# Gate and up of a decoder block: seven half-size products for each pair of tiles in place of eight

## The chip, the cores and the metric

The kernel runs on one core of one Trainium2 chip. The metric is the device time of one execution in microseconds (us), lower is better; the number given is the median of three runs. The engines are named as the profile names them: PE (matmuls; PEld are its weight loads), DVE (VectorE), ACT (ScalarE), POOL (GpSimd), SP (which issues most transfers). Each engine works through its own list of instructions in order and waits on semaphores for the others.

## The reference

One decoder block over 512 tokens of width 1024: a first norm, one wide projection, two token mixers (a retention with decay and a softmax attention with forget gates), a gated merge and an output product, then the feed-forward part, which is what the change touches:

```python
x = x + merged @ w_out[l]
h2 = rmsnorm(x, g_ffn[l])
ff = (jax.nn.silu(h2 @ w_gate[l]) * (h2 @ w_up[l])) @ w_down[l]
x = x + ff
```

`w_gate` and `w_up` are 1024 x 2816, `w_down` is 2816 x 1024, all in float32. 2816 columns are 22 tiles of 128, or 11 pairs of tiles, for gate and for up each.

## The kernel before

All stages have features on the 128 partitions and tokens along the free axis where it helps. Every float32 factor of a product is split into a high part (a cast to fp32r, on ACT) and a low part (the float32 value less its high part, on DVE), and each product is three matmuls: high x high, high x low, low x high (`three`, issued in line L72). A weight block is loaded by SP (L143), cast by ACT (L150, `wh<-raw`) and subtracted by DVE (L151, `wl<-raw,wh`).

The parts that matter here come last in the program, one behind the other:

- **The o-stage**: four pairs of output tiles of `merged @ w_out`, each pair 48 matmuls of 128x512. Behind each tile DVE adds x (L681), ACT scales by g_ffn and casts into `xgh` (L682), DVE makes `xgl` (L683), ACT squares (L685, L688), and POOL adds the squares up into `sqs` (L689). The scaled x is not yet divided by its root mean square: that factor, `r2` (one value for each token, spread over 128 partitions), comes later, as it goes through the products unchanged.
- **Gate/up**: 22 half rounds, in turn a pair of gate tiles and a pair of up tiles, each 2 tiles x 8 blocks of 128 features x 3 = 48 matmuls of 128x512. Gate: DVE multiplies the PSUM tile by `r2` (L705), ACT takes Silu (L706). Up: DVE multiplies by `r2` (L711), POOL multiplies by the gate and writes `pf` (L712). In the first round one more matmul of ones by `sqs` makes the sums of squares in all partitions, and DVE works out `r2` on 128x512 tiles.
- **Down**: 22 blocks k; each is loaded and split, `pf[k]` is split (L740 on ACT, L741 on DVE) and goes through 24 matmuls of 128x512 into eight PSUM tiles; the last two blocks are taken tile by tile, with the output added and stored behind each tile (L751, L752).

Pools of SBUF buffers set how far ahead a load can be: raw weight blocks have two or three buffers, so a load waits for the subtraction that last read its buffer. `tile.TileContext` places instructions on each engine by its own model of when they are due; where `pinned[0]` is set, PE's matmuls keep the order in which the code names them.

## Time and profile before

| what | value |
|---|---|
| runs | 733.34, 733.04, 733.48 us (median 733.34) |
| profiled execution, its own time | 733.68 us |
| span of its profile | 731.8 us |
| o-stage, first to last matmul's start | 323.7 to 367.2 us of the span |
| gate/up | 367.2 to 607.5 us (240.3 us) |
| down and output | 607.5 us to the end |
| PE busy / DVE / ACT / POOL | 99% / 50% / 35% / 15% of the span |

A line of a group reads: source line, engine, operation, out<-in by the program's names, shapes, count, then the busy time in us and the mean ns of one, then the idle time of that engine just before these instructions and what ended it. A line of the timeline reads: start in us, duration, engine, line, operation, names, shape, count, and in brackets the idle time before it. A matmul's duration is its modelled time from issue to result; how fast matmuls follow each other is read from the differences of their starts. A line of waits reads: who waited for whom, us in total, number of waits, the longest.

### The profile page before, as it was taken

How to read it: one execution, taken by the hardware profiler on the slowest of the kernel's cores; microseconds unless marked ns; L12 is line 12 of the kernel's file. 1: busy time of each engine (PE TensorE's matmuls, PEld its weight loads, DVE VectorE, ACT ScalarE, POOL GpSimd, SP SyncE). 2: the span in 40 equal slices, each digit the busy share in tenths (PEclk: the TensorE clock that was granted, in tenths of full speed). 3: DMA queues.
4: the chain of work that ended last, by engine and by line, in shares of the span. 5: the costliest groups of instructions: out<-in, count | busy, mean ns of one | idle time of the engine just before them, and what ended most of it. 6: DMA issues, size and time to landing. Idle time of an engine off the chain costs nothing.

```text
span 731.8 us, 8835 instructions
## 1 busy us (share of the span) xinstructions
PE 724.0 (99%) x3433; PEld 594.2 (81%) x3433; DVE 363.7 (50%) x630; ACT 259.1 (35%) x389; POOL 111.7 (15%) x112
## 2 busy tenths in 40 slices
...
GB/s 280 241 123 89 79 62 90 81 134 99 86 87 30 58 113 89 89 102 212 96 139 140 89 112 88 96 106 88 103 98 86 114 88 86 108 93 88 86 0 116
DMA packets 23353, 76.20 MB, mean 104 GB/s; under 512 B 2696, under 2 KB 3080, under 8 KB 23312
## 3 DMA queue, kind: packets, MB, share of 16 engines
...
q8 instruction: 27, 0.44, 0.3%
q14 instruction: 14, 0.11, 0.0%
q10 hardware_dynamic: 144, 0.02, 0.0%
HBM read 73.52 MB, written 2.11 MB: 103 GB/s over the span
## 4 chain that ended last, share of the span: by engine, by line
PE 94%; DVE 2%; ACT 1%; DMA 1%; issue 1%; POOL 0%; DVEq 0%; SPq 0%; ACTq 0%
PE acc L72 78%; PE sc L72 8%; PE tp L72 6%; PE tp L75 2%; DVE pr L494 1%; DMA xf<-in_xT_dram 1%; DMA raw<-in_w_tok_dram 0%; POOL cb L486 0%; DVE pr L498 0%; DVE tq L473 0%; ACT pr L496 0%; DVE kl L464 0%; ACT tk L463 0%; DVE up L711 0%; DVE pl L741 0%
## 5 line engine op out<-in xcount | busy, mean ns | idle before, releaser
L150 ACT CAST wh<-raw 128x1024 fp32r<-128x1024 f32 (+1 forms) x118 | 123.8, 1052 | 378.6 <-PE acc L72 313.9
L151 DVE TENSOR_TENSOR wl<-raw,wh 128x1024 fp32r<-128x1024 f32 (+1 forms) x118 | 152.2, 1291 | 196.7 <-ACT wh L150 195.3
L72 PE MATMUL acc<-xgh,wh 128*128 128x512 f32 x352 | 137.3, 390 | 0.0
L72 PE MATMUL acc<-xgh,wl 128*128 128x512 f32 x352 | 136.9, 389 | 0.0
L72 PE MATMUL acc<-xgl,wh 128*128 128x512 f32 x352 | 136.9, 389 | 0.0
L72 PEld LDWEIGHTS acc<-xgl,wh 128*128 128x128 f32 x352 | 66.1, 188 | 14.0 <-issue 0.2
L72 PEld LDWEIGHTS acc<-xgh,wl 128*128 128x128 f32 x352 | 66.1, 188 | 13.9
L72 PEld LDWEIGHTS acc<-xgh,wh 128*128 128x128 f32 x352 | 66.1, 188 | 13.8 <-issue 0.2
L72 PE MATMUL acc<-wh,xh 128*128 128x512 f32 (+2 forms) x192 | 69.7, 363 | 0.1
L712 POOL TENSOR_TENSOR pf<-up,gt 128x512 f32<-128x512 f32 x22 | 38.3, 1758 | 199.3 <-DVE up L711 199.3
L72 PE MATMUL acc<-wh,xl 128*128 128x512 f32 (+2 forms) x192 | 68.2, 355 | 0.0
L72 PE MATMUL acc<-wl,xh 128*128 128x512 f32 (+2 forms) x192 | 68.0, 354 | 0.0
L72 PE MATMUL acc<-xh,wh 128*128 128x512 f32 x128 | 51.8, 404 | 0.0
L72 PE MATMUL acc<-xh,wl 128*128 128x512 f32 x128 | 50.0, 391 | 0.0
L72 PE MATMUL acc<-xl,wh 128*128 128x512 f32 x128 | 49.9, 390 | 0.0
L72 PEld LDWEIGHTS acc<-wh,xh 128*128 128x128 f32 x192 | 36.2, 188 | 6.1 <-issue 0.5
L72 PEld LDWEIGHTS acc<-wh,xl 128*128 128x128 f32 x192 | 36.2, 189 | 5.2
L72 PEld LDWEIGHTS acc<-wl,xh 128*128 128x128 f32 x192 | 36.2, 189 | 4.6
L72 PE MATMUL acc<-pl,wh 128*128 128x512 f32 x88 | 34.2, 389 | 0.0
L72 PE MATMUL acc<-ph,wl 128*128 128x512 f32 x88 | 34.2, 389 | 0.0
L72 PE MATMUL acc<-ph,wh 128*128 128x512 f32 x88 | 33.9, 389 | 0.0
L689 POOL TENSOR_TENSOR sqs<-sqs,sq 128x512 f32<-128x512 f32 x7 | 11.6, 1651 | 122.2 <-ACT sq L688 122.0
...
## 6 DMA issues: line engine op xcount, KB each, us to landing
raw<-in_w_gu_dram SPq DMA_DIRECT2D x44, 512.0 KB, 3.5
raw<-in_w_dn_dram SPq DMA_DIRECT2D x22, 512.0 KB, 3.5
raw<-in_w_tok_dram SPq DMA_DIRECT2D x16, 512.0 KB, 3.6
raw<-in_w_a_dram SPq DMA_DIRECT2D x16, 512.0 KB, 3.6
raw<-in_w_y_dram SPq DMA_DIRECT2D x8, 512.0 KB, 3.6
raw<-in_w_o_dram SPq DMA_DIRECT2D x8, 512.0 KB, 3.9
...
```

Source lines behind the costliest of these rows:

```text
L72: in_order(nc.tensor.matmul(o, **kw))
L75: in_order(nc.tensor.transpose(out=o, in_=src, identity=ident))
L150: nc.scalar.copy(out=h[:, :width], in_=raw[:, :width])
L151: tt(out=l[:, :width], in0=raw[:, :width], in1=f32(h)[:, :width], op=ALU.subtract)
L494: nc.vector.tensor_tensor_reduce(out=pr[:, :n], in0=cb[:, :n], in1=sc[:, :n], scale=-1.0, scalar=3e38, op0=ALU.add, op1=ALU.min, accum_out=nm)
L689: gp.tensor_tensor(out=sqs, in0=sqs, in1=sq2, op=ALU.add)
L712: gp.tensor_tensor(out=pf[:, 2 * f2 + m2, :], in0=up, in1=gts[m2], op=ALU.mult)
```

## The change

Of a pair of tiles the product is a 2x2 block product: x is cut into quarters by token half and by even or odd feature block (A11, A12, A21, A22), the weights by feature block and tile (B11 ... B22). Eight products of half size were done as 48 matmuls of 128x512. The change does seven (Strassen's scheme in Winograd's form), each over four feature blocks and three split terms, so 7 x 12 = 84 matmuls of 128x256 for a pair. With

S1 = A21 - A22, S2 = S1 - A11, S3 = A11 - A21, S4 = S2 + A12 and T1 = B12 + B11, T3 = B12 + B22, T2 = T1 + B22, T4 = T2 + B21,

the seven products are B11 by A11, T1 by S1, T2 by S2, B21 by A12, T3 by S3, B22 by S4, T4 by A22; sums of them give the four quarters of the result (the first, for one, is y + u0, with y = B21 by A12 and u0 = B11 by A11). All minus signs sit in the S's, so the weights are only added.

- **o-stage**: the evacuation writes the scaled float32 x into `fx` (eight quarter slots, L695) and not straight into a high and a low part; DVE makes S1 to S4 (L705 to L708); the high and low parts of seven slots are made by two casts (L685) and two subtractions (L686) for each pair of tiles. `sq2`, the squared tile, has one buffer in place of two.
- **Weights, `factors`**: SP loads B12 twice into the two slots of `t13` (L734, 512 KB) and the other three blocks into `raw` (L735, 768 KB); POOL issues a transfer that adds B11 and B22 onto `t13` (L736, 512 KB, once the first load has landed; two of the four sums, T1 and T3, are made so); DVE makes T2 and T4 (`t24`, L740, L741). Casts (L727) and subtractions (L728) make high and low parts of `raw` (`ah`, `al`, 128x1536), `t13` (`ch0`, `cl0`, 128x1024) and `t24` (`ch1`, `cl1`, 128x1024). `raw`, `t13`, `ah`, `al` have two buffers each, in two pools; the second pool (`fp`) lies where the o-stage's buffers were. `t24`, `ch0`, `cl0`, `ch1`, `cl1` have one.
- **Sums of products**: three PSUM tiles x, y, z per pair; between the products ACT copies 128x256 states of x and z to SBUF (u0 L765, u3 L767, u1 L770, u2 L773, and the last one L775), and DVE makes the other three quarters (L779 to L781).
- **The rest of gate/up**: gate by `r2` in one 128x1024 multiply (L816; L812 for the first), Silu 128x1024 (L817; L813 for the first); up is multiplied by the gate on DVE (L820, 128x1024); POOL does no arithmetic in this stage. `r2` comes from four 128x1 matmuls after pair 0, a short chain of DVE on 128x4, and, after pair 1, four transposes of PE that spread it (`broadcast_cols`, L233 and L75). PE's order is pinned.
- **Down**: up's factor `r2` is now multiplied here (L843, one 128x512 on DVE for each k); the buffers are those of the gate/up stage (`hl` in those of `xfh`).

```diff
-    hp = tc.alloc_tile_pool(name="hp", bufs=1, side="left")
+    hp = tc.alloc_tile_pool(name="hp", bufs=1, side="right")
...
+    HT = S // 2
...
-    xgh = xp.tile([P, NK, S], F32R, name="xgh")
-    xgl = xp.tile([P, NK, S], F32R, name="xgl")
+    xfh = [xp.tile([P, 7, HT], F32R, name="xfh", tag=f"xfh{j}") for j in range(4)]
+    xfl = [xp.tile([P, 7, HT], F32R, name="xfl", tag=f"xfl{j}") for j in range(4)]
+    wq = tc.alloc_tile_pool(name="wq", bufs=1, side="right")
+    tmp = tc.alloc_tile_pool(name="tmp", bufs=1, side="left")
+    sqs = r1
+    A11, A12, A22, S1, S2, S3, S4, A21 = range(8)
+    def split_x(j, f, lo, hi):
+        nc.scalar.copy(out=xfh[j][:, lo:hi, :], in_=f[:, lo:hi, :])
+        tt(out=xfl[j][:, lo:hi, :], in0=f[:, lo:hi, :], in1=f32(xfh[j])[:, lo:hi, :], op=ALU.subtract)
+
     for mp in range(4):
+        fx = tmp.tile([P, 8, HT], F32, name="fx", tag="fx")
         def evac_o(m2, acc):
             m = 2 * mp + m2
             xn = x1[:, m, :]
             tt(out=xn, in0=acc, in1=xn, op=ALU.add)
-            act(out=xgh[:, m, :], in_=xn, func=AF.Copy, scale=gffn(m))
-            stt(out=xgl[:, m, :], in0=xn, scalar=gffn(m), in1=f32(xgh)[:, m, :], op0=ALU.mult, op1=ALU.subtract)
+            act(out=fx[:, 0:8:7, :] if m2 == 0 else fx[:, 1:3, :], in_=xn.rearrange("p (s t) -> p s t", s=2), func=AF.Copy, scale=gffn(m))
             if m == 0:
                 act(out=sqs, in_=xn, func=AF.Square)
             else:
-                sq2 = xp.tile([P, S], F32, name="sq2", tag="sq2", bufs=2)
+                sq2 = tmp.tile([P, S], F32, name="sq2", tag="sq2")
                 act(out=sq2, in_=xn, func=AF.Square)
                 gp.tensor_tensor(out=sqs, in0=sqs, in1=sq2, op=ALU.add)
         run(feat(lambda u: w_o[mp, u], 2, mgh, mgl, evac_o))
+        split_x(mp, fx, 0, 3)
+        tt(out=fx[:, S1, :], in0=fx[:, A21, :], in1=fx[:, A22, :], op=ALU.subtract)
+        tt(out=fx[:, S2, :], in0=fx[:, S1, :], in1=fx[:, A11, :], op=ALU.subtract)
+        tt(out=fx[:, S3, :], in0=fx[:, A11, :], in1=fx[:, A21, :], op=ALU.subtract)
+        tt(out=fx[:, S4, :], in0=fx[:, S2, :], in1=fx[:, A12, :], op=ALU.add)
+        split_x(mp, fx, 3, 7)
+    B12, B11, B21, B22 = range(4)
+    wpools = [wq]
+    WT = {"raw": (3, F32), "t13": (2, F32), "t24": (2, F32), "ah": (3, F32R), "al": (3, F32R),
+          "ch0": (2, F32R), "cl0": (2, F32R), "ch1": (2, F32R), "cl1": (2, F32R)}
+    seen = {}
+    def wtile(tag):
+        n, dt = WT[tag]
+        two = tag in ("raw", "t13", "ah", "al") and len(wpools) > 1
+        i = seen.get(tag, 0)
+        seen[tag] = i + 1
+        return wpools[i % 2 if two else 0].tile([P, n, 512], dt, name=tag, tag=tag)
+    def split_to(src, tags):
+        h, l = wtile(tags[0]), wtile(tags[1])
+        nc.scalar.copy(out=h, in_=src)
+        tt(out=l, in0=src, in1=f32(h), op=ALU.subtract)
+        return h, l
+    def factors(src):
+        raw, t13, t24 = wtile("raw"), wtile("t13"), wtile("t24")
+        nc.sync.dma_start(out=t13, in_=src[:, 0:1, :].broadcast_to([P, 2, 512]))
+        nc.sync.dma_start(out=raw, in_=src[:, 1:4, :])
+        gp.dma_start(out=t13, in_=src[:, 1:4:2, :], accum_op=ALU.add)
+        blocks = raw
+        a = split_to(blocks, ("ah", "al"))
+        c0 = split_to(t13, ("ch0", "cl0"))
+        tt(out=t24[:, 0, :], in0=t13[:, 0, :], in1=blocks[:, 2, :], op=ALU.add)
+        tt(out=t24[:, 1, :], in0=t24[:, 0, :], in1=blocks[:, 1, :], op=ALU.add)
+        c1 = split_to(t24, ("ch1", "cl1"))
+        return {"B11": (a, 0), "B21": (a, 1), "B22": (a, 2), "T1": (c0, 0), "T3": (c0, 1), "T2": (c1, 0), "T4": (c1, 1)}
+    def product(o, w, slot, new, js=range(4)):
+        (h, l), i = w
+        for j in js:
+            fs = slice(j * P, (j + 1) * P)
+            for n, (st, mv) in enumerate(((h, xfh), (h, xfl), (l, xfh))):
+                first = new and j == 0 and n == 0
+                mm(o, lhsT=st[:, i, fs], rhs=mv[j][:, slot, :], start=first, stop=j == 3 and n == 2, skip_group_check=not new)
+    def half_products(w, q, early=False):
+        x, y, z = (bank(t)[:, 0:HT] for t in ("sc", "acc", "acc"))
+        u = fp.tile([P, 4, HT], F32, name="u", tag="u", bufs=2)
+        opening = ((x, w["B11"], A11), (z, w["T1"], S1), (y, w["B21"], A12))
+        if early:
+            for js in (range(3), range(3, 4)):
+                for o, f, s in opening:
+                    product(o, f, s, True, js)
+        else:
+            for o, f, s in opening[:2]:
+                product(o, f, s, True)
+        nc.scalar.copy(out=u[:, 0, :], in_=x)
+        product(x, w["T2"], S2, False)
+        nc.scalar.copy(out=u[:, 3, :], in_=z)
+        if not early:
+            product(*opening[2], True)
+        nc.scalar.copy(out=u[:, 1, :], in_=x)
+        product(x, w["T3"], S3, False)
+        product(z, w["B22"], S4, False)
+        nc.scalar.copy(out=u[:, 2, :], in_=x)
+        product(x, w["T4"], A22, False)
+        nc.scalar.copy(out=q[:, 1, :], in_=x)
+        return y, z, u
+    def quarters(q, y, z, u):
+        tt(out=q[:, 0, :], in0=y, in1=u[:, 0, :], op=ALU.add)
+        tt(out=q[:, 2, :], in0=z, in1=u[:, 1, :], op=ALU.subtract)
+        tt(out=q[:, 3, :], in0=u[:, 3, :], in1=u[:, 2, :], op=ALU.subtract)
+    ws = [factors(w_gu[0, 0])]
+    tmp.release()
     mgp.release()
-    hp.release()
+    wp.release()
     fp = tc.alloc_tile_pool(name="fp", bufs=1, side="left")
     pf = fp.tile([P, NF, S], F32, name="pf")
-        def evac_g(m2, acc):
-            gt = fp.tile([P, S], F32, name="gt", tag="fa", bufs=5)
-            tt(out=gt, in0=acc, in1=r2, op=ALU.mult)
-            act(out=gt, in_=gt, func=AF.Silu)
-            gts.append(gt)
-        def evac_u(m2, acc):
-            up = fp.tile([P, S], F32, name="up", tag="fb", bufs=5)
-            tt(out=up, in0=acc, in1=r2, op=ALU.mult)
-            gp.tensor_tensor(out=pf[:, 2 * f2 + m2, :], in0=up, in1=gts[m2], op=ALU.mult)
-        if f2 == 0:
-            waiting = []
-            for n, _ in enumerate(feat(lambda u: w_gu[0, f2, u], 2, xgh, xgl, lambda m2, acc: waiting.append(acc))):
-                if n == 9:
-                    pb = bank("tp")
-                    mm(pb, lhsT=ones, rhs=sqs, start=True, stop=True)
-            rsqrt(r2, pb, 1.0 / D, [P, S], "n2", xp)
-            for m2, acc in enumerate(waiting):
-                evac_g(m2, acc)
+    r2b = r2.rearrange("p (o t) -> p o t", o=1).broadcast_to([P, 2, S])
+    pinned[0] = True
+    for n in range(NF):
+        f2, g = n // 2, n % 2
+        if n < NF - 1:
+            ws.append(factors(w_gu[(n + 1) % 2, (n + 1) // 2]))
+        pp = pf[:, 2 * f2:2 * f2 + 2, :]
+        q = pp.rearrange("p a (s t) -> p (a s) t", s=2) if g == 0 else fp.tile([P, 4, HT], F32, name="d", tag="d", bufs=2)
+        parts3 = half_products(ws[n], q, n == 0)
+        if n == 0:
+            pb = bank("tp")
+            for t in range(NT):
+                mm(pb[:, t:t + 1], lhsT=sqs[:, t * P:(t + 1) * P], rhs=ones[:, 0:1], start=True, stop=True)
+            rstd2 = rstd1
+            rsqrt(rstd2, pb[:, 0:NT], 1.0 / D, [P, NT], "n1")
+            gate0 = q, parts3
+            continue
+        if n == 1:
+            broadcast_cols(rstd2, r2)
+            q0, parts0 = gate0
+            quarters(q0, *parts0)
+            tt(out=pp, in0=pp, in1=r2b, op=ALU.mult)
+            act(out=pp, in_=pp, func=AF.Silu)
+        quarters(q, *parts3)
+        if g == 0:
+            tt(out=pp, in0=pp, in1=r2b, op=ALU.mult)
+            act(out=pp, in_=pp, func=AF.Silu)
         else:
-            run(feat(lambda u: w_gu[0, f2, u], 2, xgh, xgl, evac_g))
-        run(feat(lambda u: w_gu[1, f2, u], 2, xgh, xgl, evac_u))
+            qq = pp.rearrange("p a (s t) -> p (a s) t", s=2)
+            tt(out=qq, in0=qq, in1=q, op=ALU.mult)
+    pinned[0] = False
...
     for k in range(NF):
-        h, l = split_w(w_dn[k])
-        ph = fp.tile([P, S], F32R, name="ph", tag="fa", bufs=5)
-        pl = fp.tile([P, S], F32R, name="pl", tag="fb", bufs=5)
+        raw = wtile("raw")
+        nc.sync.dma_start(out=raw[:, 0:2, :], in_=w_dn[k])
+        src = raw[:, 0:2, :]
+        tags = (("ch0", "cl0"), ("ah", "al"), ("ch1", "cl1"), ("ah", "al"))[k % 4]
+        h, l = (wtile(t)[:, 0:2, :] for t in tags)
+        nc.scalar.copy(out=h, in_=src)
+        tt(out=l, in0=src, in1=f32(h), op=ALU.subtract)
+        hl = xp.tile([P, 7, HT], F32R, name="hl", tag=f"xfh{k % 4}")
+        ph, pl = (hl[:, 2 * v:2 * v + 2, :].rearrange("p a b -> p (a b)") for v in range(2))
+        tt(out=pf[:, k, :], in0=pf[:, k, :], in1=r2, op=ALU.mult)
         nc.scalar.copy(out=ph, in_=pf[:, k, :])
         tt(out=pl, in0=pf[:, k, :], in1=f32(ph), op=ALU.subtract)
+        h, l = (a.rearrange("p a b -> p (a b)") for a in (h, l))
         parts.append((h, l, ph, pl))
...
+    def halves(m):
+        k, n = m.shape
+        v = m.reshape(k // 256, 2, P, n // 256, 2, P)
+        v = np.stack([v[:, 0, :, :, 1], v[:, 0, :, :, 0], v[:, 1, :, :, 0], v[:, 1, :, :, 1]])
+        return v.transpose(3, 2, 0, 1, 4).reshape(n // 256, P, 4, k // 2)
```

Three places at which the order of the instructions moved, as the built program has it.

ACT, one half round of up in the middle of gate/up. Before: the casts of four weight blocks (a gate and an up half round) and two Silu.

```order
L150 CAST wh<-raw 128x1024 x4
L706 ACTIVATE gt<-gt 128x512 x2
```

Of the change (pair n = 3; the numbers behind the names tell buffers apart):

```order
L765 COPY u<-sc 128x256
L767 COPY u<-acc 128x256
L817 ACTIVATE pf<-pf 128x1024
L770 COPY u<-sc 128x256
L727 CAST ch_3854<-t_3845 128x1024
L773 COPY u<-sc 128x256
L727 CAST ah<-raw 128x1536
L727 CAST ch_3860<-t_3846 128x1024
L775 COPY d<-sc 128x256
```

ACT has nine instructions for a half round where it had three, and the cast of the next pair's `ch0` (ch_3854) stands ahead of the copy u2 (L773), the cast of `ah` for the pair after the next behind it.

DVE at the same place. Before, a gate and an up half round:

```order
L705 TENSOR_TENSOR gt<-acc,r_3088 128x512 x2
L151 TENSOR_TENSOR wl<-raw,wh 128x1024
L711 TENSOR_TENSOR up<-acc,r_3088 128x512 x2
L151 TENSOR_TENSOR wl<-raw,wh 128x1024 x2
```

Of the change, from `r2` on the gate of pair 2 to the low part of `t24` for pair 4:

```order
L816 TENSOR_TENSOR pf<-pf,r_3087 128x1024
L740 TENSOR_TENSOR t_3846<-t_3845,raw 128x512
L741 TENSOR_TENSOR t_3846<-t_3846,raw 128x512
L779 TENSOR_TENSOR d<-acc,u 128x256
L728 TENSOR_TENSOR cl_3855<-t_3845,ch_3854 128x1024
L780 TENSOR_TENSOR d<-acc,u 128x256
L781 TENSOR_TENSOR d<-u 128x256
L728 TENSOR_TENSOR al<-raw,ah 128x1536
L728 TENSOR_TENSOR cl_3861<-t_3846,ch_3860 128x1024
```

The subtraction of `al` for the pair after the next (128x1536) now stands ahead of that of `cl1` (cl_3861), which the next pair's second product needs.

DVE at the start of the stage, from the end of pair 0 to the end of pair 1 (buffer numbers shown: al_3463, cl0_3467, cl1_3473 belong to pair 1; al_3596, cl0_3600, cl1_3606 to pair 2; al_3733 to pair 3). This piece has no counterpart before.

```order
L728 TENSOR_TENSOR al_3596<-raw_3589,ah_3595 128x1536
L728 TENSOR_TENSOR al_3463<-raw_3456,ah_3462 128x1536
L728 TENSOR_TENSOR cl0_3467<-t13_3457,ch0_3466 128x1024
L728 TENSOR_TENSOR cl1_3473<-t24_3458,ch1_3472 128x1024
...
L233 TENSOR_SCALAR rb_3707<-ones_87,rstd1_86 128x128
L779 TENSOR_TENSOR d_3609<-acc_3611,u_3613 128x256
L728 TENSOR_TENSOR cl0_3600<-t13_3590,ch0_3599 128x1024
L780 TENSOR_TENSOR d_3609<-acc_3612,u_3613 128x256
L781 TENSOR_TENSOR d_3609<-u_3613 128x256
L728 TENSOR_TENSOR al_3733<-raw_3726,ah_3732 128x1536
L728 TENSOR_TENSOR cl1_3606<-t24_3591,ch1_3605 128x1024
L233 TENSOR_SCALAR rb_3710<-ones_87,rstd1_86 128x128
L233 TENSOR_SCALAR rb_3713<-ones_87,rstd1_86 128x128
```

The low part of pair 2 (al_3596) stands ahead of that of pair 1 (al_3463), and the last two of the four small multiplies that the transposes read (rb, L233) stand behind the low parts of pairs 3 and 2.

17 lines of the change are left out of this document (7 added, 10 removed).

## The prediction

> **What bounds the kernel now.** I read the page's shares, then the chain of waits, then busy time by stretches.
>
> ```profile
> PE 724.0 (99%) x3433; PEld 594.2 (81%) x3433; DVE 363.7 (50%) x630; ACT 259.1 (35%) x389; POOL 111.7 (15%) x112
> PE 94%; DVE 2%; ACT 1%; DMA 1%; issue 1%; POOL 0%; DVEq 0%; SPq 0%; ACTq 0%
> 367.23:607.49 240.26, 240.26 (x1060) 198.58 (x1059) 101.12 (x105) 64.96 (x76) 38.67 (x22) 1.00 0.33 103
> 607.49:728.20 120.71, 120.14 (x529) 98.83 (x527) 42.76 (x50) 29.01 (x37) 3.00 (x2) 1.00 0.24 79
> PE tp L72 <- DVE pl L741: 0.5, 1, 0.5
> ```
>
> The third row (gate/up) and the fourth (down) give start and end, length, busy time of PE, PEld, DVE, ACT, POOL, granted clock, share of the DMA engines, GB/s. PE is busy for all of its 240.26 us, DVE for 42%, ACT for 27%; from here to the end PE waits once for DVE, 0.5 us at the step to the down stage. PE alone bounds this stage, and the stage is as long as its matmuls are:
>
> ```profile
> 500.05 0.39 PE L72 MATMUL acc<-xgh,wh 128*128 128x512 f32 x1
> 500.27 0.39 PE L72 MATMUL acc<-xgl,wh 128*128 128x512 f32 x1
> 77.31 0.28 PE L72 MATMUL acc<-wl,xh 128*128 128x256 f32 x1
> 83.17 0.28 PE L72 MATMUL acc<-wh,xl 128*128 128x256 f32 x1
> ```
>
> A 128x512 matmul takes 240.26 / 1060 = 0.2267 us, a pair's 48 take 10.88. The last two rows are the second and the last of 51 matmuls of 128x256, each with weights of its own: 5.86 us over 49 steps, 0.120 each.
>
> **The change, part by part.**
>
> *Products.* 22 x 84 x 0.120 = 221.8 us against 240.3: **-18.5**, if PE never waits. A pair is then 10.08 us, in which ACT and DVE have more to do. Their prices:
>
> ```profile
> L150 ACT CAST wh<-raw 128x1024 fp32r<-128x1024 f32 x116 | 121.6, 1051 | 372.2 <-PE acc L72 307.5 <-issue 48.9 <-DMA raw<-in_w_gu_dram 7.6
> L740 ACT CAST ph<-pf 128x512 fp32r<-128x512 f32 x22 | 13.4, 617 | 1.7 <-POOL pf L712 1.7
> L513 ACT COPY pT<-tp 128x256 f32<-128x256 f32 x8 | 2.9, 361 | 1.8 <-PE tp L75 1.8
> 651.36 0.39 PE L72 MATMUL acc<-pl,wh 128*128 128x512 f32 x1
> 651.78 1.05 ACT L150 CAST wh<-raw 128x1024 fp32r<-128x1024 f32 x1 [3.87 <-PE acc L72]
> 652.87 1.23 DVE L151 TENSOR_TENSOR wl<-raw,wh 128x1024 fp32r<-128x1024 f32 x1 [3.62 <-ACT wh L150]
> 654.01 0.68 DVE L741 TENSOR_TENSOR pl<-pf,ph 128x512 fp32r<-128x512 f32 x1
> L751 DVE TENSOR_TENSOR ot<-acc,x 128x256 f32<-128x256 f32 x2 | 0.8, 420 | 0.7 <-PE acc L72 0.7
> 609.74 0.50 PE L72 MATMUL tp<-pl,wh 128*128 128x512 f32 x1 [0.51 <-DVE pl L741]
> 610.08 0.39 PE L72 MATMUL tp<-ph,wl 128*128 128x512 f32 x1
> ```
>
> ACT: 1.05 for 1024 elements a partition, 0.62 for 512, so an estimate of 1.49 for 1536; 0.36 for a 128x256 copy. DVE: 1.23, 0.68, an estimate of 1.78 for 1536, 0.42 for 256 with PSUM. From matmul to ACT pass 0.03 us (651.75 to 651.78), from ACT to DVE 0.04; to PE I take 0.05, and a PE that waited loses 0.11 more (next start 0.34 later, not 0.23). Instructions of one engine overlap by some 0.09 (DVE's second row starts at 654.01, the first ends at 654.10).
>
> For a pair DVE has 1.78 + 3 x 1.23 + 3 x 0.68 + 3 x 0.42 = 8.8 us, ACT 1.49 + 2.5 x 1.05 + 5 x 0.36 = 5.9. Both fit, but DVE nearly fills the period, so the order decides. With these prices I followed the five lists instruction by instruction. In the steady state, t from a pair's first matmul:
>
> - ACT casts `ch0` of the next pair from 7.28, when its last reader T3 is through, to 8.33; the copy u2 stands behind it, 8.24 to 8.60, and T4, due at 8.64, needs the bank that u2 empties: it starts 0.12 late. Period 10.20, **+2.5** over 21 pairs.
> - `ah` for two pairs on may be cast when B22 has read the old one: 8.72 to 10.21. DVE subtracts `al` behind it, to 1.81 of the next period, and `cl1`, queued behind `al`, to 2.94. T2's third matmul needs it at 3.12: with 0.16 to reach PE, 0.02 us are left. I put it at nothing, as the schedule closes; once the cover is gone each 0.1 us more costs 0.1 in about 20 pairs, 2 us.
> - `r2` on gate, its product with up (L816, L820), the sums for T2 and T4, and the two L843 of every second pair lie between 2.85 and 8.3, where nothing on PE waits for DVE. These cost nothing; the down stage saw DVE busy for 43 of 121 us, and loses no time by having L843 earlier. POOL's twenty-two multiplies go; none was on the path.
>
> *The opening.* Behind the last o-stage matmul:
>
> ```profile
> L681 DVE TENSOR_TENSOR x<-acc,x 128x512 f32<-128x512 f32 x8 | 5.4, 690 | 11.0 <-PE acc L72 8.0 <-DMA x<-in_xT_dram 2.9
> L682 ACT ACTIVATE xgh<-x,ce 128x512 fp32r<-128x512 f32 x8 | 5.7, 714 | 0.0
> L688 ACT ACTIVATE sq<-x 128x512 f32<-128x512 f32 x7 | 4.3, 618 | 0.0
> L689 POOL TENSOR_TENSOR sqs<-sqs,sq 128x512 f32<-128x512 f32 x7 | 11.6, 1651 | 122.2 <-ACT sq L688 122.0
> ```
>
> The two additions of x, two scalings and one square end at 2.13; the second square waits for POOL to free the single `sq2` (1.65 us) and ends at 3.9; only then ACT casts the first three slots (to 4.6) and DVE subtracts them (to 6.0), and four slots more (to 7.1). PE has 27 matmuls, 3.24 us, that need nothing of this, then waits 1.55 + 1.24 + 0.78, and 0.72 for u1: **+4.3**.
>
> *Pair 0 to pair 1.* Four products with one column for the norm: the nearest row is the float32 128x128 L75; an estimate of 1.0 us, bounds 0.2 and 2. `ah` of pair 2 is cast before that of pair 1 (13.0 to 14.5, then to 15.9), and DVE's list has the first step of the norm, which waits for these products (15.8), ahead of `al` of pair 2 (16.3 to 18.1) and of pair 1 (to 19.7). PE waits 0.7 + 3.6. **+5.3**.
>
> *Pair 1 to pair 2.* PE's pinned list has the transposes ahead of pair 2; the last two multiplies that feed them (L233) stand on DVE behind `al` of pair 3 and `cl1` of pair 2, which wait for pair 1's B22. PE waits 3.3; transposes 0.24. **+3.6**.
>
> *Into down.* ph, the cast of the first block and pl come behind the last up multiply: 1.3 us of waits against 0.5 + 0.1 before: **+0.7**.
>
> *The adding transfer.* No such row exists.
>
> ```profile
> raw<-in_w_gu_dram SPq DMA_DIRECT2D x44, 512.0 KB, 3.5
> cl<-in_c_late_dram SPq DMA_DIRECT2D x1, 896.0 KB, 11.9
> 13.00:30.00 17.00, 17.00 (x76) 14.05 (x76) 10.12 (x21) 8.83 (x14) 0.00 (x0) 1.00 0.97 384
> SPq L143 <- DVE wl L151: 506.0, 102, 12.9
> ```
>
> Bounds 3.5 (a plain load of its size) and 11.9 (a larger one behind others). A pair moves 512 + 768 + 512 KB in 10.2 us, some 180 GB/s, where this core moved 384 (last number of the third row); loads had slack (SP waited for buffers, not for data). By the schedule it is hidden up to 9 us; from 9 to 12.5 each us lengthens the step from pair 0 to 1 by as much; from about 12.5 on it is late for every pair, some 11 us in all for each us. I take 6, nearer the plain load: nothing.
>
> Sum: -18.5 + 2.5 + 4.3 + 5.3 + 3.6 + 0.7 = -2.1. Profiled 733.68 - 2.1 = 731.6; the median of the runs is 0.34 below the profiled time, so **731.2 us**.
>
> **Rivals.**
>
> *B, slower: the conversion chain B22, ah, al, cl1, T2 sets the period.* For it: a margin of 0.02 us, and DVE's durations are not firm:
>
> ```profile
> 369.65 2.45 DVE L683 SCALAR_TENSOR_TENSOR xgl<-x,ce,xgh 128x512 fp32r<-128x512 f32 x2
> 369.76 3.50 POOL L689 TENSOR_TENSOR sqs<-sqs,sq 128x512 f32<-128x512 f32 x2 [7.57 <-ACT sq L688]
> L151 DVE TENSOR_TENSOR wl<-raw,wh 128x1024 fp32r<-128x1024 f32 x46 | 61.5, 1338 | 85.4 <-ACT wh L150 84.2
> ```
>
> In gate/up the subtraction took 1.34, not 1.23, on the mean; beside POOL far more (two 128x512 operations took 2.45, where a 128x512 subtraction takes 0.68). Against it: POOL's arithmetic is gone. At 1.34 `al` and `cl1` are 0.27 longer, 0.25 a pair beyond the margin, 5 us in all: 736. From 0.15 to 0.5 a pair: 734 to 741. It decides from 0.10 us a pair beyond my schedule: then the gain is spent.
>
> *C: the adding transfer lands late.* POOL issues it, and POOL and DVE slowed each other above, with DVE now busy for 86% of each period. Landing at 12 us costs 3 to 7, 734 to 738; 14 us gives about 757. Against it stand the loads' 3.5. By the Trainium skill, "SBUF — State Buffer", section "SBUF: two separate sides", a transfer issued from GpSimd can stall while VectorE holds a port pair that both use, since GpSimd writes its descriptors; no run here shows it, and the sum does not rest on it.
>
> *D, better: waits smaller than worked out.* If ACT and DVE overlap more than 0.09 at the handovers and u2 comes 0.12 sooner, the 2.5 goes; if half of the 13 us of the first three pairs is hidden, 6 go: 723 to 728.
>
> *E: PE runs slowly after its two long waits.* From the o-stage's end on PE had no wait over 0.5 us, and now gets two of 3.3 and 3.6.
>
> ```profile
> 1.18 3.70 PE L72 MATMUL tp<-warm 128*128 128x512 bf16 x9 [1.18 <-DVE warm L103]
> ```
>
> At the start, after idling, nine 128x512 matmuls took 3.70 us, 0.41 each against 0.2267 later: 1.7 us lost. Twice that: 734.6. That a wait of this length is enough no row shows. The Trainium skill, "TensorE: Matmul & The Clock Gate", section "Why this matters for your kernels", says that a gap of over some 3 us drops the clock; by it E would hold, and the trace, whose granted clock is 1.00 in every stretch, has no gap to test it.
>
> **How the numbers follow.** About 0.2%, 1.5 us, is what a measurement can tell from no change: same is 731.9 to 734.8. The schedule as worked out (728 to 734) 46%: of it 0.29 faster, 0.15 same, 0.02 slower. B 22%: 0.03 same, 0.19 slower. C 9%: 0.01 same, 0.08 slower. D 13%, faster. E 10%: 0.02 faster (where D's gains meet it), 0.05 same, 0.03 slower. Sum: faster 0.44, same 0.24, slower 0.32. The range of 8 in 10 runs from 724, most of D, to 741, the end of B; 728 to 734 is the forecast's own.
>
> **What would show it.** Matmuls of 128x256 in gate/up 0.120 apart, and a period of 10.2; 0.12 before T4, ended by u2 (L773); at T2's third matmul no wait for cl1 (a wait there is B); before pair 0's later blocks, pair 1 and the transposes waits of about 4, 4 and 3.3 us; DVE's 128x1024 operations at 1.23; POOL's transfers landing under 9 us (over it is C); a granted clock of 1.00 behind the waits (less, or matmuls 0.24 apart, is E). The forecast is wrong if the matmuls are further apart than 0.120 (0.125 alone costs 9 us), or if the steady period lies above 10.4.

## The result and the profile after

The changed kernel took **747.32 us** (median; 744.82 to 748.17) against 733.25 for the kernel before in the same session: ratio **1.018**, 95% interval 1.0162 to 1.0198. The forecast was 731.2, with a range of 724 to 741; the change is slower than the kernel before by 14 us. The profiled execution has a span of 745.0 us, 13.2 more than before.

Page of the profile after: shares, granted clock by slices, chain of waits, transfers of the stage.

```profile
PE 718.3 (96%) x4235; PEld 625.8 (84%) x4235; DVE 459.5 (62%) x782; ACT 334.6 (45%) x519; POOL 94.8 (13%) x112
PEclk9999999999999999999977999999999999999999
PE 73%; DVE 10%; DMA 8%; issue 4%; ACT 3%; POOL 1%; DVEq 0%; SPq 0%; POOLq 0%; ACTq 0%
raw<-in_w_gu_dram SPq DMA_DIRECT2D x22, 768.0 KB, 5.7
t<-in_w_gu_dram SPq DMA_DIRECT2D x22, 512.0 KB, 6.8
t<-in_w_gu_dram POOLq DMA_DIRECT2D x22, 512.0 KB, 8.8
```

PE was 94% of the chain and is 73%; DVE and transfers have 18%. The clock, full in every slice before, is at 0.7 in two. The adding transfer lands after 8.8 us, and the plain 512 KB load beside it after 6.8, where a 512 KB load took 3.5 before.

Stretches of the profile after (length; busy time of PE, PEld, DVE, ACT, POOL; granted clock; DMA share; GB/s): pair 0 up to its last blocks, its rest with the norm's products, pair 1 with the transposes, pair 2, ten pairs, the other nine.

```profile
368.08:375.79 7.71, 3.91 (x29) 3.30 (x27) 6.45 (x9) 4.25 (x6) 2.35 (x3) 1.00 0.01 2
375.79:389.45 13.66, 10.76 (x65) 9.89 (x66) 4.22 (x6) 5.38 (x7) 1.65 (x2) 0.75 0.55 131
389.45:411.13 21.68, 13.52 (x89) 13.00 (x89) 16.04 (x31) 7.61 (x11) 1.08 (x1) 0.75 0.52 148
411.13:422.74 11.61, 11.61 (x86) 11.51 (x86) 6.90 (x10) 6.69 (x9) 1.08 (x1) 0.87 0.50 114
422.74:524.53 101.79, 101.79 (x842) 101.22 (x841) 80.89 (x100) 57.14 (x85) 10.86 (x10) 1.00 0.68 170
524.53:619.80 95.27, 93.15 (x759) 91.43 (x757) 71.59 (x91) 51.55 (x80) 7.61 (x7) 1.00 0.64 157
```

The ten pairs of the fifth row take 10.18 us each, PE always busy: the saving is there. The first four rows are three pairs in 54.66 us; at 10.18 they would be 30.5. The gate/up stage lasts 251.7 us (368.08 to 619.8), before 240.3. PE's waits in it (timeline; in brackets idle time and what ended it):

```profile
369.67 0.39 PE L72 MATMUL sc<-xfl,ah 128*128 128x256 f32 x1 [0.60 <-DVE xfl L686]
375.79 0.38 PE L72 MATMUL sc<-xfh,ah 128*128 128x256 f32 x1 [3.07 <-ACT xfh L685]
377.56 0.58 PE L72 MATMUL sc<-xfl,ah 128*128 128x256 f32 x1 [1.39 <-DVE xfl L686]
379.03 0.58 PE L72 MATMUL acc<-xfl,ch 128*128 128x256 f32 x1 [0.46 <-DVE xfl L686]
383.49 0.39 PE L72 MATMUL sc<-xfh,ch 128*128 128x256 f32 x1 [0.46 <-ACT u L770]
389.45 0.38 PE L72 MATMUL sc<-xfh,ah 128*128 128x256 f32 x1 [0.59 <-ACT ah L727]
395.30 0.58 PE L72 MATMUL sc<-xfh,al 128*128 128x256 f32 x1 [5.34 <-DVE al L728]
410.79 0.69 PE L75 MATMUL tp<-ctab,rb 128*128 128x128 f32 x2 [2.82 <-DVE rb L233]
549.23 0.39 PE L72 MATMUL sc<-xfh,cl 128*128 128x256 f32 x1 [0.51 <-DVE cl L728]
570.40 0.39 PE L72 MATMUL sc<-xfh,cl 128*128 128x256 f32 x1 [0.55 <-DVE cl L728]
```

From 528 on every second pair waits for `cl` (the last two rows are two of five) and takes 10.7 to 11.0 us.

Where the 13.2 us of the span are: 0.85 ahead of the stage, in code that the change doesn't touch (the stage's start lies 2 us apart over the kernels of this study, 366.8 to 368.9); 11.4 in gate/up; 1.0 in down and output. Against the forecast of 237.5 for gate/up, 14.2 too many: 11.1 in the first three pairs, 3.1 in the late waits. From the starts of PE's rows, the three pairs are:

| part of 54.66 us | forecast | measured |
|---|---|---|
| 252 matmuls at 0.120, u2 | 30.5 | 30.2 |
| waits of pair 0, with the restart behind each | 4.3 | 7.15 |
| pair 0 to pair 1: norm products, waits | 5.3 | 7.05 |
| transposes and their wait | 3.5 | 3.54 |
| matmuls slower than 0.120 | 0 | 6.7 |

The last row is the largest miss. In three stretches (377.6 to 382.9, 395.3 to 400.2, 411.1 to 414.3) matmuls follow each other 0.21 apart. The three stretches of the profile that are at half clock from end to end, then one microsecond within the second and one behind the third:

```profile
376.54:383.37 6.83, 5.01 (x20) 4.42 (x20) 2.62 (x4) 2.10 (x4) 0.00 (x0) 0.50 0.44 112
390.20:400.44 10.24, 5.14 (x24) 5.14 (x25) 9.77 (x20) 2.78 (x5) 0.00 (x0) 0.50 0.40 131
410.68:414.09 3.41, 3.30 (x16) 3.29 (x17) 2.68 (x5) 0.60 (x2) 1.08 (x1) 0.50 0.25 17
396.00:397.00 1.00, 1.00 (x7) 1.00 (x7) 1.00 (x2) 0.00 (x0) 0.00 (x0) 0.50 0.52 80
415.00:416.00 1.00, 1.00 (x11) 1.00 (x10) 0.00 (x0) 0.99 (x2) 0.00 (x0) 1.00 1.12 301
```

The granted clock is 0.50 while PE waits for `al` and for 5 us behind, with seven matmuls started per microsecond; the last row shows eleven at full clock. The matmuls of the three stretches lost 2.0, 2.35 and 1.4 us, 5.8 of the row's 6.7; the rest are u2 and single matmuls right behind a wait. The stretches last two, three and one times 3.41 us, and their starts lie 13.66 and 20.48 us apart, four and six times 3.41: the clock here changes in steps of 3.41 us.

**Why pair 0 waits** (DVE, POOL and ACT around the o-stage's last matmul, at 368.0):

```profile
368.67 0.95 DVE L686 TENSOR_TENSOR xfl<-fx,xfh 128x768 fp32r<-128x768 f32 x1
369.86 1.23 DVE L686 TENSOR_TENSOR xfl<-fx,xfh 128x1024 fp32r<-128x1024 f32 x1 [0.24 <-ACT xfh L685]
371.00 1.28 DVE L694 TENSOR_TENSOR x<-acc,x 128x512 f32<-128x512 f32 x2
375.13 1.51 DVE L708 TENSOR_TENSOR fx<-fx 128x256 f32<-128x256 f32 x1
375.09 1.27 POOL L701 TENSOR_TENSOR r<-r,sq 128x512 f32<-128x512 f32 x1 [0.74 <-ACT sq L700]
374.38 0.63 ACT L700 ACTIVATE sq<-x 128x512 f32<-128x512 f32 x1 [0.76 <-POOL r L701]
374.92 0.81 ACT L685 CAST xfh<-fx 128x768 fp32r<-128x768 f32 x1
```

The last two additions of x (L694) start at 371.0, 3 us after the matmul they need: DVE is still at the quarters of the tile pair before, which stand ahead. A 128x256 subtraction takes 0.42 with POOL idle; L708, begun beside POOL's sum, takes 1.51 and ends 0.28 behind it. The cast that PE waits for stands behind the second square, which waits for POOL (the single `sq2`).

**Why pair 1 waits** (who waited for whom, then SP, POOL and DVE):

```profile
SPq L734 <- DVE xfl L686: 19.6, 1, 19.6
379.11 0.38 SPq L734 DMA_DIRECT2D t<-in_w_gu_dram  x1
384.64 1.08 POOL L736 DMA_DIRECT2D t<-in_w_gu_dram  x1 [8.28 <-issue]
390.42 0.69 DVE L740 TENSOR_TENSOR t<-t,raw 128x512 f32<-128x512 f32 x1 [3.32 <-DMA t<-in_w_gu_dram]
391.82 3.42 DVE L728 TENSOR_TENSOR al<-raw,ah 128x1536 fp32r<-128x1536 f32 x2
```

The loads of the second buffers stand behind the last subtraction of `xfl` (SP waits 19.6 us for it): pool `fp` lies where `fx` was. They leave at 379.11; load and adding transfer take till 390.42, and DVE has L740, which reads the sum, ahead of the `al` that PE waits for.

### The profile page after: what moved, and what is told of

The parts are those of the page before. It is cut to its first block, busy times and chain, and to the rows that moved or that the text cites. A ratio compares the mean times of both kernels' runs of the same rounds, so it can differ in the third digit from the quotient of the medians.

```text
span 745.0 us, 10770 instructions
## 1 busy us (share of the span) xinstructions
PE 718.3 (96%) x4235; PEld 625.8 (84%) x4235; DVE 459.5 (62%) x782; ACT 334.6 (45%) x519; POOL 94.8 (13%) x112
## 4 chain that ended last, share of the span: by engine, by line
PE 73%; DVE 10%; DMA 8%; issue 4%; ACT 3%; POOL 1%; DVEq 0%; SPq 0%; POOLq 0%; ACTq 0%
PE acc L72 46%; PE sc L72 20%; PE tp L72 5%; DMA t<-in_w_gu_dram 5%; DVE cl L728 2%; PE tp L75 2%; DVE pr L494 1%; DVE al L728 1%; DMA out_dram<-ot 1%; POOL cb L486 1%; DMA xf<-in_xT_dram 1%; DVE fx L708 1%; DVE t L741 1%; ACT fx L695 1%; DMA raw<-in_w_gu_dram 1%
## 5 line engine op out<-in xcount | busy, mean ns | idle before, releaser
L150 ACT CAST wh<-raw 128x1024 fp32r<-128x1024 f32 (+1 forms) x52 | 54.5, 1050 | 122.8 <-PE acc L72 97.6
L151 DVE TENSOR_TENSOR wl<-raw,wh 128x1024 fp32r<-128x1024 f32 (+1 forms) x52 | 66.2, 1274 | 47.7 <-ACT wh L150 47.6
L72 PE MATMUL sc<-xfh,ch 128*128 128x256 f32 x264 | 77.5, 293 | 0.5 <-ACT u L770 0.5
L72 PE MATMUL sc<-xfh,cl 128*128 128x256 f32 x264 | 75.6, 286 | 2.1 <-DVE cl L728 2.1
L72 PE MATMUL sc<-xfl,ch 128*128 128x256 f32 x264 | 75.1, 284 | 0.0
L727 ACT CAST ch<-t 128x1024 fp32r<-128x1024 f32 x44 | 46.2, 1049 | 53.8 <-PE sc L72 43.0
L728 DVE TENSOR_TENSOR cl<-t,ch 128x1024 fp32r<-128x1024 f32 x44 | 53.7, 1222 | 16.9 <-ACT ch L727 16.9
L72 PEld LDWEIGHTS sc<-xfh,cl 128*128 128x128 f32 x264 | 50.9, 193 | 3.1 <-DVE cl L728 3.1
L72 PEld LDWEIGHTS sc<-xfh,ch 128*128 128x128 f32 x264 | 51.0, 193 | 2.0 <-ACT u L770 0.8
L72 PEld LDWEIGHTS sc<-xfl,ch 128*128 128x128 f32 x264 | 51.1, 194 | 0.0
L72 PE MATMUL acc<-xfh,ah 128*128 128x256 f32 x176 | 49.9, 284 | 0.0
L736 POOL DMA_DIRECT2D t<-in_w_gu_dram x22 | 24.0, 1093 | 201.2 <-DMA t<-in_w_gu_dram 73.6
```

The lines of the kernel that those rows point to most:

```text
L72: in_order(nc.tensor.matmul(o, **kw))
L150: nc.scalar.copy(out=h[:, :width], in_=raw[:, :width])
L151: tt(out=l[:, :width], in0=raw[:, :width], in1=f32(h)[:, :width], op=ALU.subtract)
L727: nc.scalar.copy(out=h, in_=src)
L728: tt(out=l, in0=src, in1=f32(h), op=ALU.subtract)
L736: gp.dma_start(out=t13, in_=src[:, 1:4:2, :], accum_op=ALU.add)
```

## The experiments

My theory after this reading: the loss is in three places, the opening (order on DVE and ACT, then the clock), the late buffers of pair 1 (then the clock), and a loop of load and adding transfer that fills its buffers' period. Rivals: PE's clock alone; the adding transfer alone; DVE's extra work. The diffs are excerpts; `...` stands for lines of an edit that are left out. All ratios are against the kernel before, run in the same session (medians 734.79 for e1 to e4, 733.63 for e5 to e8, 734.45 for e9 to e12, 733.83 for e13 to e15).

| kernel | us | ratio, 95% interval |
|---|---|---|
| the change | 747.32 | 1.018 (1.0162 to 1.0198) |
| e1_no_add | 736.70 | 1.0036 (1.0024 to 1.0049) |
| e2_keep_busy | 741.68 | 1.010 (1.0076 to 1.0123) |
| e3_early_buffers | 736.80 | 1.0028 (1.0013 to 1.0043) |
| e4_four_columns | 740.84 | 1.009 (1.0075 to 1.0105) |
| e5_norm_out | 746.03 | 1.0164 (1.0129 to 1.0198) |
| e6_squares_last | 744.49 | 1.0141 (1.0123 to 1.0159) |
| e7_three | 733.32 | 0.9999 (0.9983 to 1.0015) |
| e8_five | 739.07 | 1.007 (1.0044 to 1.0096) |
| e9_squares_pinned | 744.06 | 1.0133 (1.0118 to 1.0148) |
| e10_four | 733.39 | 0.9988 (0.9977 to 0.9998) |
| e11_all | 728.08 | 0.993 (0.9903 to 0.9957) |
| e12_waits | 761.63 | one run, with waits put in |
| e13_norm_later | 729.74 | 0.9943 (0.9921 to 0.9965) |
| e14_u2_first | **725.15** | **0.9885** (0.9865 to 0.9905) |
| e15_norm_back | 727.48 | 0.9917 (0.9892 to 0.9942) |

### One cause each: e1 to e4

```diff
e1_no_add
-        gp.dma_start(out=t13, in_=src[:, 1:4:2, :], accum_op=ALU.add)
```

> The changed kernel without the adding transfer (POOL's L736 left out, so T1 and T3 are only B12 and the products with them are not the reference's). Theory 1 (the loss against the forecast is made in the first three pairs, by data that come late there and by PE's half rate behind the waits): pair 1's wait falls from 5.3 us to about 1, as t13 is there some 6 us earlier, its slow stretch of 2.2 us goes, and the small waits for cl1 late in the stage (0.2 to 0.55 each, some 3 us in all) go; the wait of 3 us ahead of pair 0's last block and that of 2.8 ahead of the transposes stay: 737 to 740 us. Rival (the adding transfer is behind the whole loss): 731 to 734 us, no wait over 1.5 us left.

Transfers of the stage in e1:

```profile
raw<-in_w_gu_dram SPq DMA_DIRECT2D x22, 768.0 KB, 4.2
t<-in_w_gu_dram SPq DMA_DIRECT2D x22, 512.0 KB, 3.9
```

Without the adding transfer the loads land after 4.2 and 3.9 us. Pair 1 waits 2.61 instead of 5.34, the late waits are gone, the period is 10.19; the transposes' wait (2.77) stays. T1 and T3 lack their addition here, so e1 gives times and no usable result. The transfer and what it does to the loads beside it is worth some 10 us (1.018 to 1.0036), and yet the change without it is not faster than the kernel before: the rest is the opening.

```diff
e2_keep_busy: products into an unused bank, ahead of pair 0's last blocks (25), of pair 1 (46) and of the transposes (25)
+    def keep_busy(count):
+        idle = bank("tp")[:, 0:HT]
+        for _ in range(count):
+            mm(idle, lhsT=xfl[0][:, 0, 0:P], rhs=xfh[0][:, 0, :], start=True, stop=True)
...
```

> PE gets spare matmuls (25, 46 and 25 of 128x256 into a bank that nobody reads) ahead of pair 0's last block, ahead of pair 1 and ahead of the transposes, so that it works while it would have waited. Theory (PE's clock falls behind a wait of about 3 us, three times, 54 matmuls at 0.21 instead of 0.12: 4.7 us): the slow stretches go, 741 to 743 us against 747, though PE has 11 us more work. Rival (matmuls are slow there for another reason, new weights or contention): slow stretches stay where they are, 747 to 750.

The slow stretches behind pair 1's wait and behind the transposes' are gone; the one in pair 0 stays, where waits of 1.40 and 0.84 us are left. The ratio falls from 1.018 to 1.010, some 6 us. Of these the clock's share is what the three pairs give, 3.3 us in the profile (51.4 for 54.7), though PE does 96 matmuls more in them: slow clock is a cost of its own, on top of the waits. The rest lies ahead of the stage (1.0) and in late waits (one of 1.30 in place of five).

```diff
e3_early_buffers: u, d and ot in a pool of their own, so that the second buffers of raw, t13, ah, al lie clear of fx
+    fq = tc.alloc_tile_pool(name="fq", bufs=1, side="left")
-        u = fp.tile([P, 4, HT], F32, name="u", tag="u", bufs=2)
+        u = fq.tile([P, 4, HT], F32, name="u", tag="u", bufs=2)
...
e4_four_columns: four buffers for rb in place of two
-            rb = sm.tile([P, P], F32, name="rb", tag="rb")
+            rb = (more if more and t > 1 else sm).tile([P, P], F32, name="rb", tag="rb", bufs=2)
...
```

> u, d and the output tiles get a pool of their own above fp, so that fp no longer overlaps the o-stage's fx and sq2 and pair 1's loads wait for the last o-stage matmul, not for the last low part of x (11 us later). Theory 1: loads of pair 1 start at about 368 in place of 379 us, its wait falls from 5.3 to under 1 us and the slow stretch behind it goes: 739 to 742 us. Rival (the adding transfer takes too long wherever it starts): the wait stays at 3 or more, 744 to 747.

> Four buffers in place of two for the columns that the transposes read, so that the last two no longer stand on DVE behind the low parts of pairs 3 and 2. Theory: the wait of 2.8 us ahead of pair 2 and the slow stretch of 1.4 behind it go: 742 to 744 us. Rival (pair 2 has to wait for its own weights as long): 746 to 748.

Pair 1's first load in e3, on SP:

```profile
368.55 0.38 SPq L734 DMA_DIRECT2D t<-in_w_gu_dram  x1
```

It leaves at 368.55 and not at 379.11, and in e3 pair 1 waits for nothing; the transposes' wait (2.81) stays. The three pairs take 45.0 us where they took 54.7, and the ratio falls by 1.5 points, 11 us: the largest single cause, the place of a pool (it overlaps with e1's 10, as both shorten pair 1's wait). In e4 the transposes' wait and its slow stretch are gone, and pair 1's wait stays (4.96). The ratio falls by nearly 1 point, 7 us; in the profile the three pairs give 3.7 of it (50.9 for 54.7, the wait of 2.82 and the slow stretch behind it), and the rest lies in fewer late waits, ahead of the stage and between executions. Both have a few late waits (1.01, 0.85, 0.34 us).

### The norm factor and the squares: e5 to e10

```diff
e5_norm_out: r2 multiplied into the down stage's output, once, in place of L843 for each k
-        tt(out=pf[:, k, :], in0=pf[:, k, :], in1=r2, op=ALU.mult)
-            tt(out=ot[:, cs], in0=accs[m][:, cs], in1=x1[:, m, cs], op=ALU.add)
+            tt(out=ot[:, cs], in0=accs[m][:, cs], in1=r2[:, cs], op=ALU.mult)
+            tt(out=ot[:, cs], in0=ot[:, cs], in1=x1[:, m, cs], op=ALU.add)
e6_squares_last: the squares behind the quarters in the code (sq2 in r2's buffer, fx with two buffers)
-                sq2 = tmp.tile([P, S], F32, name="sq2", tag="sq2")
-                act(out=sq2, in_=xn, func=AF.Square)
-                gp.tensor_tensor(out=sqs, in0=sqs, in1=sq2, op=ALU.add)
+                act(out=r2, in_=x1[:, m, :], func=AF.Square)
+                gp.tensor_tensor(out=sqs, in0=sqs, in1=r2, op=ALU.add)
...
e7_three: e3, e4 and e5 together
```

> The changed kernel with up's norm factor moved once more: r2 is multiplied on the eight output tiles and not on pf (22 L843 go; eight multiplies of 128x512 come in the tail, the last one, some 0.5 us, on the path). Theory 1 (the small waits for cl1 late in the stage come because the two L843 stand on DVE between the landing of the adding transfer and the low part of t24): these waits, some 3 us in all, go, the opening stays as it was: 11 to 12 us above the kernel before in place of 14. Rival (the adding transfer alone is too late there, whatever DVE does): the waits stay, 14 to 15 above.

> The changed kernel with the squares behind the casts of the x slots in the code (the squared tile in r2's buffer, free until pair 1) and two buffers for fx. Theory (the last x block is late because ACT's cast stands behind a square that waits for POOL's sum, DVE's S4 runs beside POOL's sums, and fx has one buffer): the wait of 3.1 us ahead of pair 0's last block falls to 1.5 or less and the slow stretch behind it goes: 9 to 12 us above the kernel before in place of 14. Rival (the chain of x, scale, S1 to S4, cast and subtraction is that long by itself): the wait stays over 2.5, 13 to 15 above.

> Early buffers for pair 1, four columns for the transposes and the norm factor on the output together. Theory 1 (separate causes): 10.5 + 4 + 3 us less than the changed kernel, 2 to 5 us below the kernel before; left are the waits ahead of pair 0's last block and one slow stretch. Rival (what one mend frees another wait takes): at or above the kernel before.

e5: the late waits remain without L843 (late pairs of 10.28 to 11.21 us), which is the rival's forecast, and the tail is 2.8 us longer (128.0 for 125.3 us behind the stage). e6 doesn't test what it was for: the scheduler set the squares ahead of the casts on ACT all the same, and the wait stays (3.04). e7 is where the kernel before is (0.9983 to 1.0015): a period of 10.19 in every pair, no late waits; left are pair 0's waits (3.07, 1.19, 0.46, 0.46) and a stretch at half clock there (373.5 to 380.3).

```diff
e8_five: e7, e6's order, and pair 0 in seven PSUM tiles, three feature blocks of all products ahead of the fourth
+            a, b, c, e = (bank(t)[:, 0:HT] for t in ("sc", "acc", "acc", "tp"))
+            own = opening + ((a, w["T2"], S2), (b, w["T3"], S3), (c, w["B22"], S4), (e, w["T4"], A22))
+            for js, order in ((range(3), (0, 2, 6, 1, 3, 4, 5)), (range(3, 4), (0, 2, 6, 1, 3, 4, 5))):
+                for i in order:
+                    product(*own[i], True, js)
...
e9_squares_pinned: the change, with both squares made to follow the second cast on ACT
+                after(act(out=sq2, in_=x1[:, m, :], func=AF.Square), cast)
...
e10_four: e7 and e9, and four output buffers
```

> The three mends of the run before it with the squares last, and pair 0 with a PSUM tile of its own for each of its seven products, so that PE has 63 matmuls (7.6 us) in place of 27 (3.2 us) that need nothing of the last x block. Theory 1: no wait over 1.5 us and no slow stretch in the first three pairs, 8 to 11 us below the kernel before. Rival (pair 1's adding transfer is then the next to be late): a wait of 2 to 5 us ahead of pair 1's second product, 3 to 7 below.

> The changed kernel with ACT's order fixed by hand: the two squares of each pair of o-stage tiles come behind the cast of the slots S1 to S4, so POOL's sums come later too. Theory (the last x block is late by ACT's squares, which wait for POOL's sum, and by POOL's sums beside DVE's S1 and S4): the wait ahead of pair 0's last block falls from 3.1 to 1.5 us or less and x is complete some 2 us earlier: 10 to 12 us above the kernel before in place of 14. Rival (DVE comes to the last two x additions late, 2.8 us behind their matmuls, and that alone sets it): the wait stays over 2.5, 13 to 14 above.

> Early buffers, four columns, the norm factor on the output, the squares behind the casts, and four buffers in place of two for the output tiles (two multiplies and adds for a tile had made the tail some 2.5 us longer with two). Theory: 4 to 8 us below the kernel before; no wait over 2 us left in the stage, at most one slow stretch. Rival (the opening's wait stays, as it is set by the o-stage's DVE): 1 to 3 below.

e8: with seven tiles PE has 63 matmuls that need only the first three tile pairs, and pair 0 waits just 0.60 and 0.82; but DVE's list comes out another way (L740, waiting for the adding transfer, ahead of `al`; the norm's chain between later steps), and pair 1 waits 2.84, the transposes 6.53: worse than e7. e9: the wait falls from 3.07 to 2.33, and 2.10 us for a copy of `u`, now behind the squares on ACT, take its place. e10 is level with e7, but from two parts: its four output buffers take 2.4 us off the tail (125.7 for 128.1), and its stage is 2.3 us longer (237.2 for 234.8). Moving the squares moved the wait and gained nothing beside the other mends.

### All of it, and the clock by itself: e11 and e12

```diff
e11_all: e10, pair 0 in seven PSUM tiles (as e8), sq2 in r2's buffer, and on DVE al ahead of the sums for T2 and T4, the columns rb ahead of pair 3's al
+        if behind is not None:
+            after(low, behind)
+        after(tt(out=t24[:, 0, :], in0=t13[:, 0, :], in1=blocks[:, 2, :], op=ALU.add), low)
...
e12_waits: e7, with a chain of n copies on ACT that one small product waits for, ahead of pairs 6, 9, 12, 15
+        links = {5: 6, 8: 11, 11: 16, 14: 26}.get(n, 0)
...
```

> The same, with a PSUM tile for each of pair 0's seven products (63 matmuls ahead of the last x block), the low part of a pair's raw blocks ahead of its sums T2 and T4 on DVE, and the four columns ahead of pair 3's low part. Theory: pair 1's wait of 2.8 and the transposes' of 6.5, which the run with five mends showed, go with the two orders; no wait over 1.5 and no slow stretch: 8 to 12 us below the kernel before. Rival (pair 1's data come through the adding transfer too late for a pair 0 without waits): a wait of 2 to 4 at pair 1, 4 to 7 below.

> The kernel with early buffers, four columns and the norm factor on the output, with four waits put into PE's order on purpose, ahead of pairs 6, 9, 12 and 15: a small matmul that needs a chain of 6, 11, 16 and 26 casts of 128x64 on ACT (some 1.2, 2.3, 3.3 and 5.3 us). Theory (the clock falls behind a wait of some 3 us, and a shorter one costs only itself): matmuls 0.12 apart behind the first two, 0.21 apart for some 5 us behind the last two. Rival (any wait of over 1 us does it, so that the small waits would matter too): slow stretches behind all four. Other rival (the slow stretches belong to the first pairs' new data, not to the waits): none of the four.

PE's waits in e11 from the o-stage on, all there are up to the down stage:

```profile
379.66 1.21 PE L72 MATMUL tp<-ones,r 128*128 128x1 f32 x8 [1.69 <-POOL r L713]
392.82 0.92 PE L75 MATMUL tp<-ctab,rb 128*128 128x128 f32 x4 [0.30 <-DVE rb L235]
399.69 0.39 PE L72 MATMUL sc<-xfh,ch 128*128 128x256 f32 x1 [0.22 <-ACT u L787]
```

The three pairs take 36.5 us (54.7 in the change), the kernel 728.08: the product saving shows once the opening has no holes. The wait for the norm's last sum is still followed by slow matmuls (13, from 381 to 383).

e12, the forced waits of 2.75, 4.17, 5.51 and 9.13 us (longer than the 1.2 to 5.3 that were planned, so none is short), and the 3.5 us of PE's work from the end of each (columns as above; of the waits the first has its row):

```profile
442.60 0.42 PE L72 MATMUL tp<-slow,xfl 128*128 128x64 f32 x1 [2.75 <-ACT slow L829]
442.50:446.00 3.50, 3.40 (x16) 3.40 (x17) 2.54 (x4) 0.27 (x2) 1.09 (x1) 0.53 0.19 73
479.00:482.50 3.50, 3.37 (x19) 3.37 (x20) 1.14 (x2) 1.42 (x3) 1.09 (x1) 0.64 0.34 40
517.00:520.50 3.50, 3.42 (x16) 3.42 (x17) 0.00 (x0) 0.27 (x2) 0.66 (x1) 0.50 0.69 160
558.80:562.30 3.50, 3.47 (x18) 3.47 (x18) 0.00 (x0) 0.29 (x1) 0.00 (x0) 0.56 1.01 200
```

Each wait is followed by a clock of 0.50 to 0.64 over these 3.5 us, and the pair behind takes 11.56, 11.74, 11.83 and 11.48 us for 10.18: **1.3 to 1.65 us each, whatever the wait's length**. That is the price that rival E had put at 1.7, and the steps of 3.41 us can explain why the length does not matter: in e12 too a stretch at half clock lasts 3.41, 6.83 or 10.24 us, and the starts lie 68.27, 37.55, 34.13 and 37.55 us apart, 20, 11, 10 and 11 steps. Behind the wait of 4.17 PE had some 0.7 us of matmuls 0.12 apart before the drop (479.95 to 483.36); behind that of 9.13 the clock had been down since 551.63, and came back at 561.87. Whichever wait it was, PE then worked at half clock for 3.0 to 3.8 us, about one step.

In gate/up every wait of 2.33 us or more had a drop within it or within 2.6 us of its end. How short a wait escapes wasn't measured by a scale: waits of 1.61 (e15) and 1.69 (e11), each with the eight one-column products of the norm behind it, did not escape, nor did 1.39 us with others close by (pair 0 above; 1.40 and 0.84 in e2); 1.53 in e13 and 1.52 in e14 did. Where a wait falls among the steps may decide it; no run here varies that alone.

### What was left: e13 to e15

Open were what makes the late waits for `cl`, and what still lies between e11 and the products' gain.

```diff
e13_norm_later: e11, the norm's four products behind pair 1's first product
+            if between is not None:
+                between()
...
e14_u2_first: e13, ACT's cast of the next pair's ch0 made to follow the copy u2
+            after(cast, behind)
...
e15_norm_back: e11, with r2 multiplied into pf for each k again, as in the change
+        tt(out=pf[:, k, :], in0=pf[:, k, :], in1=r2, op=ALU.mult)
-            tt(out=ot[:, cs], in0=accs[m][:, cs], in1=r2[:, cs], op=ALU.mult)
```

> On top of e11_all the four products for the norm stand behind pair 1's first product instead of behind pair 0, so that POOL's last sum has 1.4 us more. If the 1.69 us wait and the 13 slow matmuls behind it (some 1.2 us) are what is left of the opening, both go: 2 to 3 us below e11_all, no granted clock of 0.50 in the stage, three pairs (pair 0 to pair 2) in 33.5 to 34.5 us instead of 36.5. If the transposes, whose factors then come 1.2 us later, take the wait over, a wait of 1 to 2 us for rb stands ahead of them and the gain is under 1 us.

> On top of e13_norm_later ACT copies u2 ahead of the cast ch0 of the next pair. If the 0.10 us of each period is u2 alone, the period becomes 10.08 instead of 10.18: 2 us less over the stage. Rival: ch0, and with it cl0 and what stands behind cl0 on DVE, comes 0.4 us later, so T1's third matmul or T2's waits instead: period 10.2 or more, no gain or a loss of 1 to 3 us.

> e11_all with the norm factor of up multiplied in the down stage again (one 128x512 on DVE for each k), as in the change. If the late pairs of the change came from DVE alone (two of these multiplies between t24's sum and cl1 in every second period), they come back: periods of 10.5 to 11.0 in every second pair, waits of 0.3 to 0.5 us for cl, 728 + 3 = 731 or more. If they came from the loop of t13 (load and adding transfer 17.3 us in the change, 13.5 in e11_all), the period stays at 10.18 to 10.25 throughout and the time within 1 us of e11_all.

e13: the wait of 1.69 and the slow stretch are gone (clock 1.00 throughout), and yet the three pairs take 36.4 us, not 34: pair 1 now waits itself, as all of it comes sooner.

```profile
384.08 0.39 PE L72 MATMUL acc<-xfh,cl 128*128 128x256 f32 x1 [1.53 <-DVE cl L732]
386.21 0.38 PE L72 MATMUL sc<-xfh,cl 128*128 128x256 f32 x1 [0.43 <-DVE cl L732]
568.02 0.39 PE L72 MATMUL sc<-xfh,ch 128*128 128x256 f32 x1 [0.69 <-ACT u L793]
573.05 0.39 PE L72 MATMUL sc<-xfh,cl 128*128 128x256 f32 x1 [0.22 <-DVE cl L732]
```

The last two rows are late waits, in a kernel with no L843 at all. e15, which has L843, shows one of 0.97 at 551.83; e1, which has L843 and no adding transfer, has none. What goes with them is the transfers. Landings of the plain 512 KB load and of the adding transfer from 500 to 550 us:

| kernel | load | adding transfer | sum | late waits |
|---|---|---|---|---|
| the change | 7.6 | 9.3 | 16.9 | five, 0.21 to 0.55 |
| e13 | 8.0 | 9.2 | 17.2 | 0.18 to 0.69, its last pairs 2.9 us longer in all |
| e15 | 7.9 | 8.9 | 16.8 | 0.97 |
| e11 | 5.6 | 8.1 | 13.7 | none |
| e14 | 5.7 | 7.9 | 13.6 | none |

The other kernels with the adding transfer agree: e7, e10 and e12, with sums of 13.1 to 13.9, have no late waits, and the rest, with 15.7 to 17.5, all have some.

A buffer of `t13` is loaded, added to, read by DVE and ACT and then loaded again, once in two periods, 20.4 us; with 17 of them for transfers there is no slack, with 13.7 there is. In the change the loads of one buffer start 20.36 us apart from 422 us up to the load at 513.8, and 20.91 to 21.16 apart from there on; in e14 they stay at 20.32. So the late waits go with this loop, and DVE's extra multiplies are not needed for them (e5 and e13 have late waits without L843). That L843 helps to set them off is not excluded: both kernels with early buffers that keep it (e3, e15) have late waits, and of the seven without it only e8 and e13 have. In the change the sum grew along the stage, from 4.1 + 6.8 (400 to 450 us) to 16.9. What sets it to grow in one execution and not in another of nearly the same kernel stays open: each kernel here has one profile, and e11's runs alone spread from 725.4 to 731.1, the profiled one being the fastest.

e14 has the best time of all, 725.15, 8.7 us below the kernel before: no late waits, and a period of 10.16. The copy u2 no longer holds PE, but the gain of 0.10 did not come, since T2's third matmul now holds PE by 0.09, the rival's way. Most of what e14 is ahead of e13 (4.6 us) are thus e13's late waits, which its edit is not shown to have removed. PE's rows in one pair of the change (u2's stall: the second row 0.02 late, the third 0.10) and then of e14 (the third row 0.09 late):

```profile
461.80 0.28 PE L72 MATMUL acc<-xfh,al 128*128 128x256 f32 x1
461.94 0.38 PE L72 MATMUL sc<-xfh,ch 128*128 128x256 f32 x1
462.16 0.28 PE L72 MATMUL sc<-xfl,ch 128*128 128x256 f32 x1
```

```profile
457.98 0.28 PE L72 MATMUL sc<-xfl,ch 128*128 128x256 f32 x1
458.09 0.37 PE L72 MATMUL sc<-xfh,cl 128*128 128x256 f32 x1
458.30 0.28 PE L72 MATMUL sc<-xfh,ch 128*128 128x256 f32 x1
```

In e14's gate/up 228.8 us pass (368.56 to 597.35), 11.5 fewer than before; some 2.8 are given back, 1.3 ahead of the stage and 1.5 in down and output, where two operations replace one at the end.

## Why the prediction was wrong, step by step

The steady state came as forecast in the first ten pairs behind the opening. Of the two signs by which I would have called the forecast wrong, matmuls more than 0.120 apart came only at half clock, and a period above 10.4 only late in the stage (10.18 and 10.7 to 11.0 in turn). Both look at the steady state, and most of the miss lay in the first three pairs.

- **Products, -18.5: right.** Matmuls of 128x256 follow each other 0.120 apart.
- **u2, 0.12 a pair, period 10.20: right**, 0.12 and 10.18. **The margin of 0.02 ahead of T2's third matmul: right too.** The chain B22, `ah`, `al`, `cl1` did not lose time by itself (DVE took 1.22 and 1.76 as priced), which takes B's reason away; with u2's 0.12 gone in e14, it was late by 0.09.
- **The opening, +4.3: wrong, 7.15.** I let the two additions of x start at the last o-stage matmul and end with scalings and a square at 2.13. They start 3 us late: the step left out DVE's backlog from the tile pair before, and L708 stretched by POOL's sum from 0.42 to 1.51. The held square, the single `sq2`, was foreseen. By the Trainium skill, "SBUF — State Buffer", section "SBUF: two separate sides", a VectorE operation with two SBUF inputs and a GpSimd operation that reads SBUF lock each other out for a whole instruction; the rows agree (L708 ends 0.28 us behind POOL's sum).
- **Pair 0 to pair 1, +5.3: wrong, 7.05.** The norm products were right (0.95 for 1.0). The wait for `al` was 5.34, not 3.6: the prediction has no wait for the loads of pair 1 in it, and they left at 379.11, 11 us behind the o-stage's last matmul and behind the last `xfl`, because a pool lies on `fx`; then came a longer adding transfer with L740 behind it ahead of `al`. e3 takes this wait away whole.
- **Pair 1 to pair 2, +3.6: right**, 2.82 and restart, 3.54; e4 shows that the two buffers of `rb` were the reason.
- **Into down, +0.7: right in kind**, 0.73 of wait; the part behind the stage is 1.0 longer.
- **The adding transfer, 6 us, hidden up to 9: wrong.** It took 8.8, so by my own bound it was hidden, and yet late waits came. The larger fault is "loads had slack": the plain loads, 3.9 and 4.2 us without it, take 6.8 and 5.7 beside it. C counted its landing alone, and what the late waits go with is the loop of load and addition. They cost 3.1 us; that C's 3 to 7 has this number is chance, as C asked it for a landing at 12 us (and its 757 for 14 us is some 5 more than its own prices add up to). The transfer has its part in pair 1's wait too (5.34, 2.61 without it in e1).
- **The clock, nothing in the sum: wrong, 5.8 us.** Rival E, at 10%, had place, mechanism and price: waits of a few microseconds are followed by a half clock. It had two drops at 1.7; there were three, of 2.0, 2.35 and 1.4, as pair 0 has a cluster of waits (3.07, 1.39, 0.46). The Trainium skill, "TensorE: Matmul & The Clock Gate", section "Why this matters for your kernels", asks for no idle gap of over some 3 us between matmuls. Here single waits of 2.75 (e12) and 2.82 us were enough. So I should have taken E into the forecast for both of its waits, of 3.6 and 3.3 us.

The failed steps added up: of 15 us between the forecast and the measured span, 5.8 are the clock, 4.6 the longer waits of the first pairs, 3.1 the late waits, and some 1.7 are the stage's later start, the end, and single matmuls behind waits. No one of them would have taken the kernel out of the range; I had put the clock and the adding transfer at nothing in the sum and made a rival of each, and priced no case in which they come together with longer waits.
